# Output and down projections with the activations stationary and 512 weight columns moving, in a two-layer hybrid decoder trunk

## The chip, the cores and the metric

The kernel runs on one core of one Trainium2 chip. The metric is the device time of one execution in microseconds (us); the time before is the median of three runs. A difference of less than about 0.3% (7.8 us here) is about what such a measurement cannot tell from no change.

## What is computed

Two layers over 256 tokens of 2048 channels. Each layer mixes tokens (three groups of heads behind one input projection and one output projection), then channels (a gated MLP with a short causal convolution). The two projections of this case are the ones that bring a sub-layer's result back to 2048 channels, each followed by an RMSNorm over the channels, a gate and the residual sum:

```python
mix = jnp.concatenate([o_a, o_b, o_c], axis=-1) @ w_out[l]          # (256, 2048) @ (2048, 2048)
x = x + gate1 * rmsnorm(mix, mix_post_norm[l])
h = rmsnorm(x, ffn_pre_norm[l]) * (1.0 + scale2) + shift2
u = causal_dwconv(h @ ffn_w_up[l], ffn_conv[l]) + ffn_conv_b[l]
gate_br, up = u[..., :D_FF], u[..., D_FF:]
y = (jax.nn.gelu(gate_br, approximate=True) * up) @ ffn_w_down[l]   # (256, 5632) @ (5632, 2048)
x = x + gate2 * rmsnorm(y, ffn_post_norm[l])
```

## The kernel before

**Layout and products.** Activations lie with channels on the 128 partitions and the 256 tokens along the free dimension; `x` is 16 such tiles (k = 0 to 15) in the buffers S1 and S3. Every large product is float32 made of three products of rounded halves (float32r): a weight `w` is split into `wh` and `wl`, an activation into `hh` (or `mh`) and `hl` (or `ml`), and `mm3` (L262 to L266) adds `wh·hh` (L264), `wh·hl` (L265) and `wl·hh` (L266) in PSUM. The weights are the stationary operand (128x128 blocks) and the 256 tokens move (258 where two columns for the shift ride along). So each weight block costs three loads of the stationary operand and three products of 256 columns.

**The stream of weights.** All weights come as one stream of chunks of 512 KB (128 partitions x 1024 floats), issued from the SP queue (L179) into 6 raw buffers, in the order in which `build_stream` lists them. Between them stand the chunks of the modulation's weights (`ada`, L181), which VectorE multiplies and sums (L208). A weight chunk is split by ScalarE (L202, the rounded half) and VectorE (L203, the rest) into one of 4 `hl` buffers, two chunks ahead of its use (`piece`, L544, with LOOK = 2). Epilogues are generators that advance one step per chunk (`tick`).

**The two projections.** The output projection (in `mix_layer`) runs in two halves of the sum: first the channels 8 to 15 (attention), then 0 to 7 (the delta rule), 16 chunks each; a chunk is one column of blocks (`ct`), eight blocks deep. The down projection (in `ffn_layer`) comes in three groups of 16, 16 and 12 channel tiles of the MLP, each after the up-projections that feed it; a group has 16 columns of blocks with two chunks each (8 and 8, or 8 and 4 blocks), in the order of `down_order`, which puts the first chunks of four columns ahead. `m_gen` (L761) moves each finished column from PSUM: ScalarE copies it (L766) or VectorE adds it to what is there (L768). In the last group it also squares it for the norm (ScalarE L452, the sum of squares on GpSimd L453; the last two columns apart, L777 and L780).

**The joint.** After a projection, `post` (L485) sums the squares over channels with products by a column of ones (L460), forms mean and epsilon (VectorE L468), takes the power -1/2 on GpSimd (L260), and spreads it over the partitions with a product (L308). Then `step(i)` makes, for each of the 16 tiles, `m *= rs` (VectorE L518), `x += gate * m` (VectorE L521), the next `hh` (ScalarE L525) and `hl` (VectorE L528). `h_first` (L543) calls the steps while it multiplies the first four tiles of the next projection, 48 products per four k. There are three such joints, and a tail after the last projection, where L510 and L511 do the two sums over up to four tiles at once and SP stores them (L512).

What stands in which order on an engine is decided when the program is built: the code gives the order of emission, and a scheduler moves instructions of one engine past each other within the limits of their dependences.

## Time and profile before

| | |
|---|---|
| three runs | 2584.64, 2586.0 (the median) and 2592.09 us |
| profiled execution | span 2591.2 us from the first to the last instruction; its own time is not listed beside the runs', and its span lies 5.2 us above their median and within their range |
| TensorE matmul busy, weight load busy | 2494.2 and 2416.5 us (96% and 93%) |
| VectorE, ScalarE, GpSimd busy | 2051.5, 1385.0, 176.4 us (79%, 53%, 7%) |
| mean granted TensorE clock | 0.989 |
| moved by DMA | 630.48 MB, mean 243 GB/s |

Busy time of matmuls overlaps from one to the next, and their ends are modelled; the distance from one start to the next is what a product costs in a row of them. In a timeline row the first number is the start, the second the time, in us; "x2" counts equal instructions that follow each other, and a bracket at the end gives the idle time before and what ended it. In a table of stretches a row has the stretch, its length, and then for PE, PEld, DVE, ACT and POOL the busy time in us with the count of instructions; the last three numbers are the granted share of the TensorE clock, the busy share of the DMA engines and the GB/s they moved. PE is TensorE, PEld its weight load, DVE VectorE, ACT ScalarE, POOL GpSimd, SP the queue that issues the transfers.

### The profile page before, as it was taken

The numbers are of one execution on the slowest core, as the hardware profiler recorded it, in microseconds if no ns is written. First come the engines' busy times: TensorE is split into PE (matmuls) and PEld (weight loads), VectorE is DVE, ScalarE is ACT, GpSimd is POOL, SyncE is SP. The second block draws the span as 40 slices with busy tenths as digits, with TensorE's granted clock in tenths as the row PEclk, the third lists the DMA queues.
The fourth block names the chain that finished last, engine by engine and source line by source line (L and its number), as shares of the span: only waits on it lengthen the run. The fifth ranks groups of instructions, "written<-read, shape, count | busy, mean of one in ns | idle before, by whom it ended". The sixth has DMA issues, their size and how long they took to land.

```text
span 2591.2 us, 51150 instructions
## 1 busy us (share of the span) xinstructions
PE 2494.2 (96%) x20144; PEld 2416.5 (93%) x20144; DVE 2051.5 (79%) x3828; ACT 1385.0 (53%) x2357; POOL 176.4 (7%) x208
## 2 busy tenths in 40 slices
PE   3999999989999999999989999999999999999997
PEld 2999978989999999999989998898899999999997
DVE  7888988899876888688869887678977467766764
ACT  2465356456553555345547556664656455644654
POOL 0001100230000000000121110002100000000001
PEclk9999999999999999999999999999999999999998
DMA  9997878958888888888747765587566666666653
GB/s 366 342 336 223 294 262 268 338 196 284 266 270 282 262 264 265 282 272 268 259 158 264 242 208 183 170 278 276 187 212 206 210 208 208 210 208 208 211 165 122
DMA packets 175268, 630.48 MB, mean 243 GB/s; under 512 B 19905, under 2 KB 20305, under 8 KB 174769
## 3 DMA queue, kind: packets, MB, share of 16 engines
q1 hardware_dynamic: 170784, 612.44, 71.8%
q0 software_dynamic: 4096, 14.62, 1.7%
q8 instruction: 158, 2.59, 0.4%
q14 instruction: 84, 0.69, 0.1%
q10 hardware_dynamic: 146, 0.14, 0.0%
HBM read 618.73 MB, written 8.39 MB: 242 GB/s over the span
## 4 chain that ended last, share of the span: by engine, by line
PE 61%; DMA 16%; DVE 14%; issue 7%; ACT 2%; POOL 0%; DVEq 0%; POOLq 0%; ACTq 0%
PE mm L264 17%; PE mm L266 17%; PE mm L265 17%; DMA raw<-ada 15%; DVE hl L203 5%; DVE raw L208 3%; PE mm L578 2%; DVE ys L655 1%; ACT hl L202 1%; DVE hl L528 1%; PE sd L1279 1%; DVE S L521 1%; PE sd L303 1%; ACT ys L652 1%; PE mm L1177 0%
## 5 line engine op out<-in xcount | busy, mean ns | idle before, releaser
L264 PE MATMUL mm<-hh,hl 128*128 128x258 f32 (+1 forms) x4056 | 1154.0, 286 | 33.4 <-ACT hh L433 25.2
L266 PE MATMUL mm<-hh,hl 128*128 128x258 f32 (+1 forms) x4056 | 1149.8, 284 | 11.8 <-DVE hl L203 10.8
L265 PE MATMUL mm<-hl 128*128 128x256 f32 x4056 | 1147.5, 283 | 10.3 <-DVE hl L528 7.8
L203 DVE TENSOR_TENSOR hl<-raw,hl 128x1024 fp32r<-128x1024 f32 (+1 forms) x774 | 929.7, 1205 | 231.3 <-ACT hl L202 230.1
L202 ACT CAST hl<-raw 128x1024 fp32r<-128x1024 f32 (+1 forms) x774 | 794.2, 1028 | 586.2 <-PE mm L266 469.2
L264 PEld LDWEIGHTS mm<-hh,hl 128*128 128x128 f32 x4056 | 763.8, 189 | 40.2 <-ACT hh L433 25.5
L266 PEld LDWEIGHTS mm<-hh,hl 128*128 128x128 f32 x4056 | 773.2, 191 | 21.4 <-DVE hl L203 18.2
L265 PEld LDWEIGHTS mm<-hl 128*128 128x128 f32 x4056 | 774.5, 191 | 18.8 <-DVE hl L528 13.9
L208 DVE SCALAR_TENSOR_TENSOR raw<-raw,c_bc 128x1024 f32<-128x1024 f32 x384 | 475.5, 1242 | 176.0 <-DMA raw<-ada 162.5
L266 PE MATMUL mm<-mh,hl 128*128 128x256 f32 x1920 | 544.9, 284 | 5.4 <-DVE hl L203 5.3
L265 PE MATMUL mm<-ml,hl 128*128 128x256 f32 x1928 | 546.4, 283 | 0.1
L264 PE MATMUL mm<-mh,hl 128*128 128x256 f32 x1920 | 545.6, 284 | 0.1
L266 PEld LDWEIGHTS mm<-mh,hl 128*128 128x128 f32 x1920 | 368.9, 192 | 7.2 <-DVE hl L203 7.2
L265 PEld LDWEIGHTS mm<-ml,hl 128*128 128x128 f32 x1928 | 370.6, 192 | 0.6 <-issue 0.3
L264 PEld LDWEIGHTS mm<-mh,hl 128*128 128x128 f32 x1920 | 368.9, 192 | 1.8 <-issue 1.4
L655 DVE SCALAR_TENSOR_TENSOR ys<-us,fvec,ys 128x255 f32<-128x255 f32 x352 | 168.6, 481 | 9.2
L651 ACT ACTIVATE us<-us,c 128x256 f32<-128x256 f32 x176 | 89.1, 507 | 130.9 <-DVE c L634 129.6
L453 POOL TENSOR_TENSOR t<-t 128x256 f32<-128x256 f32 x97 | 90.9, 937 | 929.8 <-ACT t L452 929.0
L652 ACT ACTIVATE ys<-us,fvec 128x256 f32<-128x256 f32 x176 | 105.6, 601 | 5.3
L633 DVE TENSOR_TENSOR us<-mm,rs 128x256 f32<-128x256 f32 x174 | 73.0, 420 | 19.7 <-PE mm L266 19.6
L316 ACT CAST mh<-ys 128x256 fp32r<-128x256 f32 x88 | 35.4, 404 | 76.2 <-DVE ys L1366 76.2
L452 ACT ACTIVATE t<-S 128x256 f32<-128x256 f32 x97 | 39.5, 410 | 50.1 <-DVE S L768 49.0
(339 smaller groups left out, 1798.5 us busy)
## 6 DMA issues: line engine op xcount, KB each, us to landing
raw<-ada SPq DMA_DIRECT2D x384, 512.0 KB, 4.7
raw<-up SPq DMA_DIRECT2D x352, 512.0 KB, 4.5
raw<-w_in SPq DMA_DIRECT2D x176, 512.0 KB, 4.8
raw<-down SPq DMA_DIRECT2D x160, 512.0 KB, 4.5
raw<-w_out SPq DMA_DIRECT2D x64, 512.0 KB, 5.3
raw<-down SPq DMA_DIRECT2D x32, 256.0 KB, 3.4
raw<-uq SPq DMA_DIRECT2D x6, 512.0 KB, 5.8
S<-xt SPq DMA_DIRECT2D x4, 512.0 KB, 10.0
```

The costliest lines, as they stand in the source:

```text
L202: nc.scalar.copy(out=hi[:, :n], in_=raw[:, :n])
L203: nc.vector.tensor_tensor(out=lo[:, :n], in0=raw[:, :n], in1=hi.bitcast(F32)[:, :n], op=ALU.subtract)
L208: self.ada_ins = nc.vector.scalar_tensor_tensor(out=raw, in0=raw, scalar=1.0, in1=self.c_bc[:, hf * 1024:(hf + 1) * 1024], op0=ALU.mult, o ...
L264: mm(ps, wh, hh, start=start, stop=False)
L265: mm(ps[:, :256], wh, hl, start=False, stop=False)
L266: mm(ps, wl, hh, start=False, stop=stop)
L453: nc.gpsimd.tensor_tensor(out=self.sqacc, in0=self.sqacc, in1=t, op=ALU.add)
L578: self.nc.tensor.matmul(ps, lhsT=cv[0][0][:, k, :], rhs=self.x[kk // 8][:, kk % 8, :], start=i == 0 and k == 0, stop=kk == 15)
L633: nc.vector.tensor_tensor(out=out[r], in0=ps[r, :256], in1=self.rs[r], op=ALU.mult)
L651: nc.scalar.activation(out=u, in_=u, func=AF.Identity, bias=b)
L652: nc.scalar.activation(out=y, in_=u, func=AF.Identity, scale=taps[:, n - 1:n], bias=bias)
L655: nc.vector.scalar_tensor_tensor(out=y[:, s:], in0=u[:, :S - s], scalar=taps[:, n - 1 - s:n - s], in1=y[:, s:], op0=ALU.mult, op1=ALU.add)
```

## The change

The weights become the moving operand and the activations the stationary one. `mm3t` multiplies, for each half T of the tokens, a 128x128 block of activations (`hi`, `lo`) by 512 columns of one row of weight blocks: three products of 512 columns per T in place of six of 256 (two column blocks, three each, per 256 columns of weights; over the same chunk 12 products in place of 24, with the same number of columns). The result is by tokens: `m[:, T, :]` has tokens on the partitions and 2048 channels along the free dimension.

- A chunk is now two blocks deep and 512 columns wide (`w_out` and `down` are laid out anew on the host, still 4 KB per partition), and the last group of the down projection has 24 full chunks in place of 16 full and 16 half ones.
- `m_gen` moves 128x512 at once; in the last group ScalarE squares each and sums it in the same instruction (`accum_out`), so that the sums of squares need neither GpSimd nor the products by ones.
- In `post` VectorE reduces the eight sums, GpSimd takes the power as before, and VectorE makes two diagonal matrices of the result (`dg`).
- `turn(k)` multiplies a 128x128 block of `m` by the diagonal in plain float32: this brings channels back to the partitions and applies the norm at once, into PSUM, two k to a buffer. `add(k)` does `x += gate * turned`; the separate `m *= rs` is gone, and in the tail each k is added alone.

```diff
+    def mm3t(self, pss, wh, wl, hi, lo, start, stop):
+
+        mm = self.nc.tensor.matmul
+        for T, ps in enumerate(pss):
+            sl = slice(T * 128, T * 128 + 128)
+            mm(ps, hi[:, sl], wh, start=start, stop=False)
+            mm(ps, hi[:, sl], wl, start=False, stop=False)
+            mm(ps, lo[:, sl], wh, start=False, stop=stop)
...
-        c = self.rs_cols([(sq, slice(0, 128)) for sq in [self.sqacc, *self.last_sqs.values()]], D)
+        c = self.col()
+        nc.vector.tensor_reduce(out=c, in_=self.msq.rearrange("p (t j) -> p t j", t=2), op=ALU.add, axis=mybir.AxisListType.X)
+        self.rs_ins = nc.vector.tensor_scalar(out=c, in0=c, scalar1=1.0 / D, scalar2=EPS, op0=ALU.mult, op1=ALU.add)
+        r = self.col()
+        self.rpow(r, c, 0)
+        dg = self.tmp()
+        for T in range(2):
+            nc.vector.tensor_scalar(out=dg[:, T * 128:T * 128 + 128], in0=self.cs("ident"), scalar1=r[:, T:T + 1], scalar2=None, op0=ALU.mult)
...
-        ps = self.sd(256)
-        self.bcast_cols(ps, c)
+        def turn(k):
+
+            if k % 2 == 0:
+                pss[k // 2] = self.sd()
+            for T in range(2):
+                o = k % 2 * 256 + T * 128
+                nc.tensor.matmul(pss[k // 2][:, o:o + 128], lhsT=m[:, T, k * 128:k * 128 + 128], rhs=dg[:, T * 128:T * 128 + 128],
+                                 start=True, stop=True)
+
+        def add(k):
+            xk = x[k // 8][:, k % 8, :]
+            return nc.vector.scalar_tensor_tensor(out=xk, in0=pss[k // 2][:, k % 2 * 256:k % 2 * 256 + 256], scalar=g[:, k:k + 1],
+                                                  in1=xk, op0=ALU.mult, op1=ALU.add)
...
         def step(i):
             if i < KT:
-                nc.vector.tensor_tensor(out=m[:, i, :], in0=m[:, i, :], in1=ps, op=ALU.mult)
+                turn(i)
             k = i - 1
             if 0 <= k < KT:
-                ins = nc.vector.scalar_tensor_tensor(out=x[k // 8][:, k % 8, :], in0=m[:, k, :], scalar=g[:, k:k + 1],
-                                                     in1=x[k // 8][:, k % 8, :], op0=ALU.mult, op1=ALU.add)
+                ins = add(k)
...
+    def by_tokens(self, ids, act, m, prev, last):
+
+        n = len(act)
+        for j in range(4):
+            pss = [self.mm(512) for _ in range(2)]
+            for i, c in enumerate(ids[j]):
                 def fn(cv):
                     wh, wl = cv[0]
+                    for k in range(2):
+                        kk = 2 * i + k
+                        self.mm3t(pss, wh[:, k, :], wl[:, k, :], *act[kk], kk == 0, kk == n - 1)
+                self.piece([c], fn)
+                if i == len(ids[j]) - 1:
+                    for T in range(2):
+                        self.spawn(self.m_gen(m, j, T, pss[T], prev, last))
                 self.tick()
...
+            self.sq_ins = nc.scalar.activation(out=ps, in_=m[:, T, sl], func=AF.Square, accum_out=self.msq[:, T * 4 + j:T * 4 + j + 1])
...
-                d = {}
-                for ct, i in down_order():
-                    k = f0 + 8 * i
-                    d[ct, i] = add(io["down"][l, ct, :, k:min(k + 8, f1), :])
-                downs.append(d)
+                downs.append([[add(io["down"][l, j, :, k:k + 2, :]) for k in range(f0, f1, 2)] for j in range(4)])
```

**The order on the engines.** On TensorE, at the end of the last down projection, before (a name is the tile written, then what it is made of: `mm` a PSUM buffer, `mh`/`ml` the halves of an activation tile, `hl` a weight buffer):

```order
L264 MATMUL mm_30209<-mh10_29425,hl_30190 128x256
L265 MATMUL mm_30209<-ml10_29426,hl_30190 128x256
L266 MATMUL mm_30209<-mh10_29425,hl_30190 128x256
L264 MATMUL mm_30209<-mh11_29440,hl_30190 128x256
L265 MATMUL mm_30209<-ml11_29441,hl_30190 128x256
L266 MATMUL mm_30209<-mh11_29440,hl_30190 128x256
L460 MATMUL sd_30254<-cst_87,t_29617 128x1
```

and with the change:

```order
L265 MATMUL mm_26928<-hl_26979,mh11_26604 128x512
L266 MATMUL mm_26928<-hl_26979,mh11_26604 128x512
L267 MATMUL mm_26928<-hl_26979,ml11_26605 128x512
L265 MATMUL mm_26929<-hl_26979,mh11_26604 128x512
L266 MATMUL mm_26929<-hl_26979,mh11_26604 128x512
L267 MATMUL mm_26929<-hl_26979,ml11_26605 128x512
```

Two blocks of one chunk took six products of 256 columns; now one row of blocks takes six of 512, three into each of two PSUM buffers (one per half of the tokens), and nothing by ones follows.

On VectorE, at the first joint (after the first output projection), before, from the last two columns' sum to the first steps:

```order
L768 TENSOR_TENSOR S_5382<-part,mm 128x256 x2
L780 TENSOR_TENSOR t<-S_5382 128x256
L397 TENSOR_TENSOR hh<-mod,hh 128x16
L203 TENSOR_TENSOR hl<-raw,hl 128x1024
L468 TENSOR_SCALAR c<-sd 128x1 x2
L203 TENSOR_TENSOR hl<-raw,hl 128x1024
L518 TENSOR_TENSOR S_5382<-S_5382,sd 128x256 x2
L521 SCALAR_TENSOR_TENSOR S_5383<-S_5382,gcol,S_5383 128x256
L518 TENSOR_TENSOR S_5382<-S_5382,sd 128x256
L521 SCALAR_TENSOR_TENSOR S_5383<-S_5382,gcol,S_5383 128x256
L528 SCALAR_TENSOR_TENSOR hl<-S_5383,acol,hh 128x256
```

and with the change (L196 is the former L203, L523 `add`, L548 the former L528):

```order
L797 TENSOR_TENSOR S_5174<-part,mm 128x512 x2
L498 TENSOR_REDUCE c<-c 128x2
L398 TENSOR_TENSOR hh<-mod,hh 128x16
L499 TENSOR_SCALAR c<-c 128x2
L196 TENSOR_TENSOR hl<-raw,hl 128x1024
L504 TENSOR_SCALAR t<-cst,c 128x128 x2
L196 TENSOR_TENSOR hl<-raw,hl 128x1024 x2
L523 SCALAR_TENSOR_TENSOR S_5175<-sd,gcol,S_5175 128x256 x2
L196 TENSOR_TENSOR hl<-raw,hl 128x1024
L548 SCALAR_TENSOR_TENSOR hl<-S_5175,acol,hh 128x256
L523 SCALAR_TENSOR_TENSOR S_5175<-sd,gcol,S_5175 128x256
```

The sums by `rs` (L518) are gone; two splits of weights now stand between the diagonal (L504) and the first `add`, and a third right behind it. At the second and third joints it is one split ahead of the first `add`, and one behind.

## Rows read from the trace of the kernel before

**Rows 1.** The page's busy times and its chain of waits by engine.

```profile
PE 2494.2 (96%) x20144; PEld 2416.5 (93%) x20144; DVE 2051.5 (79%) x3828; ACT 1385.0 (53%) x2357; POOL 176.4 (7%) x208
...
PE 61%; DMA 16%; DVE 14%; issue 7%; ACT 2%; POOL 0%; DVEq 0%; POOLq 0%; ACTq 0%
```

**Rows 2.** Table of stretches: four of the six down projections.

```profile
735.00:827.60 92.60, 92.31 (x770) 92.10 (x769) 62.13 (x81) 41.22 (x55) 0.00 (x0) 1.00 0.84 279
...
1253.00:1327.30 74.30, 70.74 (x578) 70.53 (x577) 47.90 (x76) 36.26 (x56) 12.98 (x16) 0.98 0.71 233
...
2275.60:2367.70 92.10, 92.10 (x770) 92.10 (x769) 52.92 (x63) 34.94 (x35) 0.00 (x0) 1.00 0.68 209
...
2504.80:2573.80 69.00, 69.00 (x578) 69.00 (x577) 33.35 (x50) 38.13 (x62) 9.63 (x13) 1.00 0.46 138
```

**Rows 3.** Timeline of TensorE in a down projection, ten products that follow each other.

```profile
2299.74 0.28 PE L264 MATMUL mm<-mh,hl 128*128 128x256 f32 x1
...
2300.82 0.28 PE L264 MATMUL mm<-mh,hl 128*128 128x256 f32 x1
```

**Rows 4.** Timeline of TensorE in the latent keys' and values' projection, first layer.

```profile
350.96 0.39 PE L1217 MATMUL sd<-hl,ml 128*128 128x512 f32 x1
...
352.12 0.40 PE L1219 MATMUL sd<-hl,ml 128*128 128x512 f32 x1
```

**Rows 5.** The same in the second layer.

```profile
1627.78 0.28 PE L265 MATMUL mm<-ml,hl 128*128 128x256 f32 x1
...
1628.38 0.40 PE L1217 MATMUL sd<-hl,ml 128*128 128x512 f32 x1
...
1629.31 0.28 PE L264 MATMUL mm<-ml,hl 128*128 128x256 f32 x1
```

**Rows 6.** Timeline of TensorE, plain float32 products.

```profile
190.09 0.59 PE L835 MATMUL sd<-w,cst 128*128 128x256 f32 x2
190.52 0.38 PE L836 MATMUL sd<-w,cst 128*128 128x128 f32 x2
190.74 0.39 PE L837 MATMUL sd<-w,cst 128*128 128x128 f32 x2
```

**Rows 7.** Table of stretches: the second halves of the two output projections.

```profile
488.00:531.90 43.90, 43.46 (x362) 43.25 (x362) 41.34 (x58) 22.55 (x31) 15.57 (x13) 1.00 0.93 333
...
1750.00:1800.30 50.30, 49.31 (x404) 48.49 (x403) 43.46 (x60) 22.50 (x32) 13.65 (x13) 1.00 0.92 327
```

**Rows 8.** Waits in the first layer's last down projection: total, times, longest.

```profile
PE mm L266 <- DVE hl L203: 3.6, 1, 3.6
```

**Rows 9.** Table of stretches: the first joint up to its first product, and a part behind it.

```profile
531.90:539.30 7.40, 2.94 (x19) 2.47 (x17) 5.06 (x12) 2.00 (x5) 1.61 (x1) 0.71 0.53 169
...
552.00:573.00 21.00, 17.85 (x130) 15.98 (x130) 21.00 (x31) 11.44 (x22) 7.69 (x9) 1.00 0.44 130
```

**Rows 10.** Timeline of the first joint.

```profile
534.66 1.61 POOL L260 TENSOR_TENSOR c<-c,pw 128x2 f32<-128x2 f32 x1 [3.97 <-DVE c L468]
536.32 1.22 PE L308 MATMUL sd<-cst,c 128*128 128x128 f32 x4 [2.00 <-POOL c L260]
537.58 0.75 DVE L518 TENSOR_TENSOR S<-S,sd 128x256 f32<-128x256 f32 x2 [1.87 <-PE sd L308]
```

**Rows 11.** Groups by line and shape: xcount | busy us, mean ns.

```profile
L203 DVE TENSOR_TENSOR hl<-raw,hl 128x1024 fp32r<-128x1024 f32 x742 | 907.7, 1227 | 225.1 <-ACT hl L202 223.9
...
L203 DVE TENSOR_TENSOR hl<-raw,hl 128x512 fp32r<-128x512 f32 x32 | 22.1, 692 | 6.2 <-ACT hl L202 6.2
...
L202 ACT CAST hl<-raw 128x512 fp32r<-128x512 f32 x32 | 19.7, 619 | 16.0 <-PE mm L266 15.2 <-ACT hl L202 0.5 <-ACT t L452 0.3
...
L443 DVE TENSOR_SCALAR t<-t,c 128x128 f32<-128x128 f32 x16 | 3.9, 284 | 4.0 <-POOL c L260 4.0
```

**Rows 12.** Timeline of VectorE in the tail.

```profile
2578.42 2.35 DVE L510 TENSOR_TENSOR S<-S,sd 128x1024 f32<-128x1024 f32 x2 [2.10 <-PE sd L308]
...
2587.09 0.75 DVE L511 TENSOR_TENSOR S<-S,S 128x256 f32<-128x256 f32 x2
```

93 lines of the change are left out of this document (30 added, 63 removed).

## The prediction, made before the changed kernel was run

> **What bounds the kernel now.** I read the page first, then the table of stretches, then the timelines inside a stretch. The page says that TensorE is busy for 96% of the span and holds 61% of the chain that ended last [rows 1]; since matmul busy time overlaps itself, this alone does not show a bound. The table does. In the down projections, three per layer, TensorE's busy time fills the stretch, while VectorE and ScalarE have a third or more to spare and the transfers run below 280 GB/s [rows 2]. There are 768 products in a full group and 576 in the last one, so a full group of the second layer takes 92.1 / 768 = 0.120 us per product. The timeline shows that pace as a steady beat: nine steps from 2299.74 to 2300.82 are 0.120 each [rows 3]. Nothing is waited for there. What changes the step changes the time.
>
> The joints are bounded otherwise. Some 7.4 us pass between a projection's last product and the next projection's first, in which TensorE does 2.9 us of work, at a granted clock of 0.71 [rows 9], so more than half of that stretch at the lower of its two levels, 1.2 GHz. Later, while the next operand is made tile by tile, VectorE is busy for 21.0 of 21.0 us and TensorE for 17.85 [rows 9]. So in that part VectorE is the bound.
>
> **The products.** The change takes 24 products of 256 columns from each chunk and puts 12 of 512 in their place; a pair of the old ones costs 2 x 0.1198 = 0.2396 us. The price of a new one stands in this trace, since the values of the latent attention are already made in just this way: halves of an activation stationary, 512 converted weight columns moving. Five steps from 350.96 to 352.12 make 0.232 us each [rows 4]; in the second layer four steps from 1628.38 to 1629.31 make 0.2325, and the five 256-column products right ahead of them, from 1627.78 to 1628.38, 0.120 each [rows 5]. I take 0.232, a saving of 0.0076 us per pair. As to the bounds: the single steps that I add up lie between 0.22 and 0.24; at 0.24 nothing is saved, and 0.22 would save 0.02. Plain float32 products tell the same small story from another side: one with 256 columns takes (190.52 - 190.09) / 2 = 0.215 us, two of 128 take 0.22 [rows 6].
>
> The down projections have 4224 such products, 2112 pairs: 2112 x 0.0076 = **-16 us** (0 at 0.24, -41 at 0.22). The output projections have 1536, 768 pairs: -6 if TensorE alone set their pace. But in their second halves VectorE is busy for 41.3 of 43.9 us in the first layer and 43.5 of 50.3 in the second, and the DMA engines for 0.92 to 0.93 of the time [rows 7]. I give them half: **-3 us** (0 to -6).
>
> The Trainium skill ("TensorE: Matmul & The Clock Gate", Back-to-back issue gap) gives the gap of a product at full clock as its columns over 2.4 GHz plus 2.5 ns, so that joining two saves only the 2.5 ns. The rows differ from it: both lengths run slower than it says, 256 columns by some 10 ns. By the rule's difference alone the down projections would save 5 us in place of 16.
>
> **Moving the results out** gets cheaper and stays off the path: eight moves of 128x512 per group, at about 0.69 us by a VectorE instruction of that shape [rows 11], in place of sixteen of 128x256. They are covered by VectorE's free third [rows 2]; without that cover eight of them would cost 5.5 us per group. Of the 13 GpSimd additions per last group none is left. The SP queue keeps its transfers and bytes, except that 16 pairs of a full and a half chunk become 24 full ones. In the first layer's last group the half chunks are consumed faster than they arrive with the modulation's chunks between them: one wait of 3.6 us on a split that stood behind it on VectorE [rows 8]. Equal chunks should spare part of it: **-2 us** (0 to -3.6).
>
> **The joints**, three of them. What goes: on VectorE 16 sums by `rs` per joint, two of which take 0.75 us [rows 10], so 6 us in the stretch where VectorE is the bound; on TensorE the two spreading products with their loads, 1.22 us [rows 10]. What comes: first, a longer start. The last sum is 128x512, 0.69 in place of about 0.4 us; the square stands on ScalarE, 0.62 us for that width [rows 11]; the diagonal takes two VectorE instructions of 0.28 [rows 11]; GpSimd's 1.61 us [rows 10] stays. The tiny products by ones go, which pays for most of that. Then the splits ahead of the first `add`, 1.23 us each [rows 11]: two at the first joint, one at the others, of which the turning products hide about 0.7. I put the first product with the new operand 1.7 us later at the first joint and 0.5 later at the others. These splits are moved, not added: what is done early need not be done in the full stretch. Second, 32 plain products of 128 columns on TensorE at 0.11 us each [rows 6], 3.5 us at the upper clock and twice that at the lower. Twelve stand ahead of the first product, beside the splits; the other twenty, 2.2 us, fall into the stretch where TensorE is idle for 3.1 us [rows 9], which hides them as long as VectorE is late there. With VectorE 6 us shorter TensorE comes within 1 or 2 us of being the bound itself, so most of the 6 us is not to be had. I put each joint at -1 us (-4 to +4): **-3 us**.
>
> **The tail.** VectorE's two sums ran from 2578.42 to 2587.84, 9.4 us [rows 12]. Sixteen single `add` take some 0.4 each, 6 us; TensorE, back at the lower clock, needs 2 x 0.22 per tile, 7 us in all, and becomes the slower one. That is 2.4 less, and the start is 0.3 later: **-2 us** (-3 to +1).
>
> **Sum:** -16 - 3 - 2 - 3 - 2 = -26. The profiled span of 2591.2 would become 2565; that execution lies 5.2 us over the median of the runs, 2586.0, and I hold the difference against the median: **2560 us**.
>
> **The rivals.** (A) *The columns set the pace, not the products.* 512 columns then cost what two times 256 cost, 0.24, and only stall, joints and tail are left, -7: 2579. For it: the two prices differ by only 3%, and one step in rows 4 and 5 is as long as 0.24. Against it: the mean of nine steps. The Trainium skill's rule for the gap (the page and section above) is a case of this kind: by its 2.5 ns per pair the estimate would be 2574. (B) *A fixed cost per product was hidden in the steady beat*, and 512 columns run at the shortest step seen, 0.22: -41 - 7 for the down projections, stall, joints and tail, and another -8 in the output projections, half of their 768 x 0.02: 2530. For it: a steady beat without a free step; against it the same mean. (C) *The joints take it back.* If the turning products run at the lower clock, where the granted 0.71 puts the joint [rows 9], 32 of them cost 7 us, and the twenty late ones 4.4 where 3.1 were idle; with the later start and twelve early ones uncovered this makes +5 per joint in place of -1: 2578. Against it: the clock is back at 1.00 in the stretch where most of them fall. (D) *Slower: the moving weights collide with their own making.* The 512 moving columns are read from buffers beside which ScalarE and VectorE write the next chunk, and the nine measured steps come from two single chunks, not from a full stream. At 0.25 the 2880 products cost 0.0104 x 2880 = +30 us, less 7: 2609. It decides from about 0.245, where (0.245 - 0.2396) x 2880 = 15.6 us outweigh the 7 and the 0.3% bound. Against it: the same chunks are read as stationary blocks now, beside the same writes, without a wait.
>
> **How the numbers follow.** About 0.3%, 7.8 us, is what a measurement of this kernel can tell from no change. My forecast (a step of 0.226 to 0.237, joints about even) has 0.62, with a range of its own of 2548 to 2572. A has 0.16, half of it beyond the bound; B 0.10, C 0.08, half beyond the bound, D 0.04. Faster: 0.62 + 0.08 + 0.10 + 0.04 = 0.84; within 0.3%: 0.12; slower: 0.04. The range leaves out the outer part of B, part of C and all of D: 2540 to 2579.
>
> **What the profile will show.** A down projection's full group of the second layer should take 384 x 0.232 = 89 us in place of 92.1, with steps of 0.23; if it takes 92, A holds, if 84.5, B. The span from a projection's last product to the next one's first should be near 9 us at the first joint and 8 at the others; VectorE's full stretch behind it should be shorter or TensorE full in it. The plain products of the joint should stand 0.11 us apart, or 0.22 where the clock is low. The wait of 3.6 us should be shorter, and VectorE's last sums in the tail should take 7 us in place of 9.4. I am wrong if the step of the new products is not what rows 4 and 5 show, or if a joint's first tiles take over 4 us longer than now.

## The result, and the profile after

The changed kernel takes 2549.2 us in the median of four runs (2547.18 to 2564.59); the kernel before, run beside it, takes 2586.2. The ratio is 0.986 with a 95% interval of 0.9831 to 0.9889: faster by 37 us, 11 more than forecast, inside the range of 2540 to 2579. On another chip the same kernel came to 2553.6 us and 0.9886 (0.9868 to 0.9905).

The page: TensorE's weight loads fall by 141 us of busy time, while its products are still busy for 97% of the span; GpSimd falls from 176 to 123 us, and TensorE holds 64% of the chain that ended last instead of 61% [rows 1].

```profile
PE 2464.5 (97%) x17456; PEld 2275.2 (89%) x17456; DVE 2014.4 (79%) x3724; ACT 1374.0 (54%) x2299; POOL 122.8 (5%) x156
...
PE 64%; DMA 16%; DVE 11%; issue 6%; ACT 2%; POOL 0%; DVEq 0%; POOLq 0%; ACTq 0%
```

The table of stretches, with the columns of [rows 2]: two down groups of the first layer (the first and the last), the same of the second layer, the second halves of the output projections (they answer to [rows 7]), the first joint and the stretch behind it (they answer to [rows 9]), and the tail.

```profile
729.50:819.40 89.90, 88.69 (x385) 71.30 (x384) 61.10 (x81) 40.81 (x47) 0.00 (x0) 1.00 0.85 284
1242.30:1308.90 66.60, 65.64 (x290) 53.56 (x288) 44.02 (x60) 31.22 (x44) 1.69 (x3) 1.00 0.78 258
2240.40:2327.20 86.80, 86.80 (x385) 71.92 (x384) 50.25 (x55) 35.17 (x35) 0.00 (x0) 1.00 0.72 217
2464.40:2529.50 65.10, 65.10 (x290) 53.88 (x288) 31.72 (x34) 27.19 (x36) 0.00 (x0) 1.00 0.45 130
487.00:528.00 41.00, 39.65 (x173) 31.94 (x172) 35.28 (x50) 18.43 (x26) 0.00 (x0) 1.00 0.95 342
1729.00:1771.70 42.70, 42.70 (x191) 35.34 (x189) 34.58 (x48) 19.59 (x28) 0.00 (x0) 1.00 0.96 360
528.00:538.60 10.60, 5.52 (x26) 5.12 (x25) 8.18 (x16) 5.79 (x12) 2.21 (x2) 0.72 0.56 200
551.00:573.00 22.00, 20.90 (x178) 20.70 (x177) 19.74 (x28) 11.78 (x20) 9.46 (x9) 1.00 0.60 193
2529.50:2546.70 17.20, 9.64 (x66) 8.90 (x64) 8.90 (x22) 1.40 (x4) 0.69 (x1) 0.90 0.31 122
```

The second layer's groups still have TensorE full from end to end; they are simply shorter: 86.8 us for 384 products, 65.1 for 288. The first layer's have small holes now (88.69 of 89.90 busy), which before were nearly absent (92.31 of 92.60 [rows 2]).

Where the profiled spans' 44.5 us (2591.2 to 2546.7) went, stage by stage, in both traces. A group or an output projection is taken from its first product to the start of its last; a joint with its stage runs from there to the end of the up-projections or input projection behind it:

| stage | before | after | difference |
|---|---|---|---|
| six down groups | 512.8 | 485.3 | -27.5 |
| two output projections | 199.6 | 188.5 | -11.1 |
| three joints, each with the stage behind it | 688.4 | 686.5 | -1.9 |
| tail | 17.4 | 17.2 | -0.2 |
| the rest, which the change does not touch | | | -3.8 |

The rest is mostly one stretch of the second layer's attention (74.6 to 70.4 us), which comes to anything from 70.4 to 74.6 in the runs of this study. The two profiled executions lie on opposite sides of their medians, so 44.5 between them is 37 between the medians. The rows of joints and tail are one execution each, too: in another execution of the same changed kernel (the run `again` of experiment 7) the joints with their stages come to 689.9 us and the tail to 18.6, so that for these two rows the traces show no change either way.

**The step.** Timeline of TensorE in a steady stretch of a down projection, seven products in a row:

```profile
2299.80 0.39 PE L266 MATMUL mm<-hl,mh 128*128 128x512 f32 x1
...
2301.16 0.39 PE L266 MATMUL mm<-hl,mh 128*128 128x512 f32 x1
```

Six steps in 1.36 us: 0.2267 each, not 0.232. The same timeline in the first layer, from a wait for a split on:

```profile
738.72 0.50 PE L266 MATMUL mm<-hl,mh 128*128 128x512 f32 x1 [0.47 <-DVE hl L196]
739.06 0.39 PE L267 MATMUL mm<-hl,ml 128*128 128x512 f32 x1
739.29 0.39 PE L265 MATMUL mm<-hl,mh 128*128 128x512 f32 x1
...
740.45 0.39 PE L267 MATMUL mm<-hl,ml 128*128 128x512 f32 x1
```

Here the six steps from 739.06 to 740.45 make 0.232, the price that [rows 4, 5] had shown. Those rows were the first products behind another kind of product, as these are the first behind a wait; later the steps settle at 0.2267 (from 740.67 on in this stretch).

**The first joint.** TensorE and VectorE, from the last product of the output projection to the first of the up projection:

```profile
528.01 0.39 PE L267 MATMUL mm<-hl,ml 128*128 128x512 f32 x1
533.48 5.49 PE L518 MATMUL sd<-t,S 128*128 128x128 f32 x24 [5.08 <-DVE t L504]
538.62 0.99 PE L256 MATMUL mm<-hh,hl 128*128 128x258 f32 x3
```

```profile
533.53 2.35 DVE L196 TENSOR_TENSOR hl<-raw,hl 128x1024 fp32r<-128x1024 f32 x2
535.80 0.87 DVE L523 SCALAR_TENSOR_TENSOR S<-sd,gcol,S 128x256 f32<-128x256 f32 x2
536.59 1.22 DVE L196 TENSOR_TENSOR hl<-raw,hl 128x1024 fp32r<-128x1024 f32 x1
537.72 0.48 DVE L548 SCALAR_TENSOR_TENSOR hl<-S,acol,hh 128x256 fp32r<-128x256 f32 x1
```

The twelve turning products (two records each) take 5.1 us, 0.43 each; the granted clock is 0.72 over the joint and 0.50 over the turns themselves (533.5 to 538.6). VectorE does two splits ahead of its first sum and a third ahead of its first difference. From last to first product it is 10.6 us here, 9.5 and 10.3 at the other joints; before it was 7.3 to 7.4. The stages behind give it back, 4.7, 1.1 and 4.4 us shorter. Two things differ there. From 551 us on TensorE is busy for 20.9 of 22.0 us, where it was busy for 17.85 of 21.0 [rows 9]. And in the 12 us right behind the joint the clock is higher; before and after:

```profile
539.30:552.00 12.70, 12.24 (x72) 11.44 (x72) 11.63 (x24) 7.66 (x18) 5.67 (x7) 0.76 0.13 45
```

```profile
538.60:551.00 12.40, 12.40 (x103) 12.40 (x103) 10.64 (x20) 8.18 (x18) 6.59 (x8) 0.96 0.45 151
```

Before, the clock stood at 0.50 for the first 6 us of that stretch, with TensorE and VectorE both busy throughout; now the low time falls on the turns ahead of it. What each of the two is worth was not separated.

**VectorE beside no GpSimd.** Groups of VectorE by line in the second layer's output projection, second half: the splits and the modulation products took 1.28 and 1.46 us in the kernel before and take 1.22 now. Before:

```profile
L203 DVE TENSOR_TENSOR hl<-raw,hl 128x1024 fp32r<-128x1024 f32 x16 | 20.5, 1282 | 0.0
L208 DVE SCALAR_TENSOR_TENSOR raw<-raw,c_bc 128x1024 f32<-128x1024 f32 x13 | 19.0, 1464 | 3.8 <-DMA raw<-ada 3.8
```

and after:

```profile
L196 DVE TENSOR_TENSOR hl<-raw,hl 128x1024 fp32r<-128x1024 f32 x14 | 17.1, 1223 | 0.4 <-ACT hl L195 0.4
...
L200 DVE SCALAR_TENSOR_TENSOR raw<-raw,c_bc 128x1024 f32<-128x1024 f32 x12 | 14.7, 1223 | 2.1 <-DMA raw<-ada 2.1
```

### The profile page after: what moved, and what is told of

Its sections match the earlier page's. It is cut to its first block, busy times and chain, and to the rows that moved or that the text cites. A ratio compares the mean times of both kernels' runs of the same rounds, so it can differ in the third digit from the quotient of the medians.

```text
span 2546.7 us, 45378 instructions
## 1 busy us (share of the span) xinstructions
PE 2464.5 (97%) x17456; PEld 2275.2 (89%) x17456; DVE 2014.4 (79%) x3724; ACT 1374.0 (54%) x2299; POOL 122.8 (5%) x156
## 4 chain that ended last, share of the span: by engine, by line
PE 64%; DMA 16%; DVE 11%; issue 6%; ACT 2%; POOL 0%; DVEq 0%; POOLq 0%; ACTq 0%
DMA raw<-ada 15%; PE mm L256 12%; PE mm L258 12%; PE mm L257 12%; PE mm L265 6%; PE mm L266 6%; PE mm L267 6%; DVE hl L196 4%; DVE raw L200 3%; PE mm L598 2%; DVE ys L675 1%; PE sd L518 1%; ACT hl L195 1%; PE sd L304 1%; PE sd L1299 1%
## 5 line engine op out<-in xcount | busy, mean ns | idle before, releaser
L195 ACT CAST hl<-raw 128x1024 fp32r<-128x1024 f32 x758 | 791.3, 1048 | 668.8 <-PE mm L258 276.5
L196 DVE TENSOR_TENSOR hl<-raw,hl 128x1024 fp32r<-128x1024 f32 x758 | 925.7, 1226 | 227.5 <-ACT hl L195 226.1
L200 DVE SCALAR_TENSOR_TENSOR raw<-raw,c_bc 128x1024 f32<-128x1024 f32 x384 | 469.3, 1225 | 167.5 <-DMA raw<-ada 155.3
L266 PE MATMUL mm<-hl,mh 128*128 128x512 f32 x960 | 376.0, 392 | 4.8 <-DVE hl L196 4.6
L265 PE MATMUL mm<-hl,mh 128*128 128x512 f32 x960 | 374.6, 391 | 0.0
L267 PE MATMUL mm<-hl,ml 128*128 128x512 f32 x960 | 373.9, 389 | 0.0
L266 PEld LDWEIGHTS mm<-hl,mh 128*128 128x128 f32 x960 | 180.2, 188 | 48.6 <-DVE hl L196 12.3
L265 PEld LDWEIGHTS mm<-hl,mh 128*128 128x128 f32 x960 | 180.2, 188 | 38.5 <-issue 1.4
L267 PEld LDWEIGHTS mm<-hl,ml 128*128 128x128 f32 x960 | 180.3, 188 | 36.9
L252 POOL TENSOR_TENSOR c<-c,pw 128x2 f32<-128x2 f32 x26 | 26.9, 1040 | 1180.2 <-DVE c L499 919.3
L1383 ACT ACTIVATE ys<-ys 128x256 f32<-128x256 f32 x88 | 36.6, 416 | 44.9 <-DVE ys L675 44.2
```

What stands on the lines that cost most here:

```text
L195: nc.scalar.copy(out=hi[:, :n], in_=raw[:, :n])
L196: nc.vector.tensor_tensor(out=lo[:, :n], in0=raw[:, :n], in1=hi.bitcast(F32)[:, :n], op=ALU.subtract)
L200: self.ada_ins = nc.vector.scalar_tensor_tensor(out=raw, in0=raw, scalar=1.0, in1=self.c_bc[:, hf * 1024:(hf + 1) * 1024], op0=ALU.mult, o ...
L265: mm(ps, hi[:, sl], wh, start=start, stop=False)
L266: mm(ps, hi[:, sl], wl, start=False, stop=False)
L267: mm(ps, lo[:, sl], wh, start=False, stop=stop)
```

## Experiments

My theory after the result, worked out from the two steps (0.2267 us for 512 columns and 0.120 for 256, so 0.107 for 256 columns more): every float32r product costs about 13 ns besides its columns, so that 512 columns in place of two times 256 save 13 ns per pair and nothing else in the change matters much. A line through two points always fits; experiment 2 adds a third. The rival: the exchange of the roles (fewer moves out, no GpSimd sums) is what gained. Then: why do the joints and the tail give nothing, and why did the first layer's groups gain less than the second's?

**1. Half the width (w256).**

```diff
-        for j in range(4):
-            pss = [self.mm(512) for _ in range(2)]
+        for j in range(NJ):          # NJ = D // W, W = 256
+            pss = [self.mm(W) for _ in range(2)]
```

> Roles as in the changed kernel (activation stationary, weight columns moving, norm by tokens, turned back by the diagonal), but 256 weight columns per product instead of 512: twice as many products, eight blocks of columns instead of four. Theory (a product has a fixed cost of about 13 ns beside its columns, 119.8 = 256 x 0.4167 + 13.1 and 226.7 = 512 x 0.4167 + 13.3, and the width is the whole gain): steps of 0.120 us, the second layer's full down group back at 92 us (86.8 in the changed kernel), its last one at 69, the whole 2880 x 0.0129 = 37 us over the changed kernel, less some 6 us where the first layer's waits hide it: 2579 to 2587. Rival (it is the exchange of the roles that gains: fewer moves out, a freer VectorE and GpSimd): steps of 0.113, groups stay at 87, time 2549 to 2555.

Measured: 2580.0 us, ratio to before 0.997 (0.9957 to 0.9984). Table of stretches, a full down group and the last one of the second layer:

```profile
2263.40:2355.40 92.00, 92.00 (x770) 92.00 (x769) 52.02 (x63) 34.93 (x35) 0.00 (x0) 1.00 0.67 207
...
2492.50:2561.50 69.00, 69.00 (x578) 69.00 (x576) 33.39 (x42) 29.08 (x52) 0.00 (x0) 1.00 0.41 123
```

Both groups are back to what [rows 2] had. All down and output stages together take 712.5 us, against 712.4 before and 673.8 in the changed kernel. The width is the gain there. The exchange of roles alone moves nothing in the sum of these stages: the two output projections get shorter (103.7 and 93.6 us for 105.1 and 94.5), the first layer's down groups longer by about as much. The 8 us that remain against the kernel before (2588.0 in that session) lie elsewhere, a part of them at the first joint and its stage (198.7 us for 202.9).

**2. A quarter of the width (w128)**, the same edit with W = 128.

> The same with 128 weight columns per product, four times as many products. Theory of the fixed cost: a step of 128 x 0.4167 + 13.2 = 66.5 ns, the second layer's full down group 1536 x 0.0665 = 102 us, the whole 2880 x (4 x 0.0665 - 0.2267) = 113 us over the changed kernel, about 2660. Rival (the step has a floor, because a block of 128 columns has to be loaded as stationary for each product and that takes as long as 256 columns move): 0.12 per product, a full group near 184 us, the whole some 730 us longer, near 3280.

Measured: 3874.7 us, ratio 1.4963 (1.49 to 1.5026). A stretch of the first layer's second down group and one of the second layer's first, then the product with which TensorE goes on in the former after a wait, and two products from the latter:

```profile
1473.60:1784.10 310.50, 308.36 (x1446) 308.21 (x1446) 69.80 (x104) 32.84 (x33) 0.00 (x0) 0.50 0.27 85
3088.00:3249.40 161.40, 161.40 (x1448) 161.40 (x1447) 41.35 (x38) 37.96 (x61) 0.00 (x0) 1.00 0.37 113
```

```profile
1475.72 0.33 PE L268 MATMUL mm<-hl,mh 128*128 128x128 f32 x1 [2.42 <-ACT mh L320]
...
3149.89 0.28 PE L270 MATMUL mm<-hl,ml 128*128 128x128 f32 x1
...
3150.78 0.28 PE L269 MATMUL mm<-hl,mh 128*128 128x128 f32 x1
```

Eight steps in 0.89 us are 0.111 each at the upper clock. "Columns and 13 ns" fails below 256 columns: 128 cost nearly as much as 256 (0.120), so there is a floor near 0.11, as the rival said (whether it is the load of the stationary block or the rate of narrow products, these rows do not tell). Between 256 and 512 the theory agrees with the steps from which it was worked out and with experiment 1; for other widths it is not shown. Both forecasts of the total were far too short, as neither had the clock: in five of the eight down and output stages it is granted at 0.50 for all or most of the time, and such a full group takes 320 us in place of 171. In each of the five TensorE first waited for an operand, 1.6 to 2.4 us in four (the line at 1475.72 is one), 7.0 in the output projection of the first layer (which had a low stretch before that, too, behind three waits of 0.8 to 0.9 us); the clock fell then, and came back only when the stage's products had ended, though TensorE was busy. The three stages without such a wait stayed at 1.00.

**3. Keep TensorE at work through the joints (warm).** Unread products stand behind the last one:

```diff
+                    if last and j == 3 and i == len(ids[j]) - 1:
+                        spare = self.sd()
+                        with self.tc.issue_after(self.pe_ins.ins):
+                            for _ in range(22 if self.w_last + 1 < len(self.widx) else 14):
+                                self.nc.tensor.matmul(spare, act[0][0][:, :128], wh[:, 1, :], start=True, stop=True)
```

> The changed kernel with products that nobody reads between a projection's last product and the first turning product: 22 of 512 columns at each of the three joints, 14 at the tail (their sums go to a spare PSUM buffer). They keep TensorE at work until the diagonal is ready. Theory (the turns are slow because TensorE stood still and runs at the lower clock): the granted clock of the joints rises from 0.72 to 0.9 or more, a turning product takes 0.11 to 0.22 us instead of 0.43, twelve of them end 2.5 us earlier; first products 1 to 1.8 us earlier at the first joint and 0.5 to 1 at the others, the tail's first sums 1.4 us earlier: 4 to 6 us faster than the changed kernel, 2543 to 2546. Rival (VectorE, with the splits ahead of its first sums, sets the start, and the slow turns only fill its time): the turns get faster and the first products come at the same time, gain at most 2 us, all of it in the tail: 2547 to 2549. Second rival (the turns are slow for another reason, their loads or plain float32): clock up, turns still 0.4 apart.

Measured: 2553.9 us, ratio 0.9857 (0.9838 to 0.9876), beside 0.986 and 0.9886 of the changed kernel. Stretches of the first and third joint, and TensorE's timeline in the third (L787 are the unread products):

```profile
532.90:541.10 8.20, 8.10 (x49) 6.86 (x47) 5.76 (x13) 5.39 (x11) 1.53 (x1) 1.00 0.51 185
...
1780.00:1787.80 7.80, 7.80 (x49) 6.90 (x47) 5.71 (x13) 4.49 (x10) 1.59 (x1) 1.00 0.33 101
```

```profile
1780.21 5.15 PE L787 MATMUL sd<-hl,mh 128*128 128x512 f32 x22
1785.20 2.84 PE L518 MATMUL sd<-t,S 128*128 128x128 f32 x24
1787.79 0.48 PE L256 MATMUL mm<-hh,hl 128*128 128x258 f32 x2
```

The clock stays at 1.00, the twelve turns take 2.6 us (0.22 each) in place of 5.1, and the joints 8.2, 7.8 and 7.8 us in place of 10.6, 9.5 and 10.3. So the turns were slow because of the clock, and they did stand on the path. But only the third joint clearly keeps its gain (joint and stage together 196.6 in place of 198.9). The first gives it back behind (200.9 for 201.4). For the second it cannot be told: 286.4 for 286.2, but 290.3 in the other execution of the changed kernel. The tail takes 15.6 us in place of 17.2 (18.6 in the other execution). That is some 4 us of stages, too little for the total to tell; the total lies above both expected ranges, in a session in which the kernel before took 2588.0. The second rival (slow for another reason than the clock) is out: with the clock up the turns halve.

**4. Fewer turns ahead of the first product (few).**

```diff
-            while n < 4 * kg + 6:
+            while n < (4 * kg + 6 if kg else 4):
                 step(n)
...
                 for k in range(4):
                     kk = 4 * kg + k
+                    while n < kk + 4:
+                        step(n)
+                        n += 1
```

> The changed kernel with four tiles turned ahead of the first product of the next projection instead of six (the other turns stand between the products of the first four k), and with the split of the third chunk behind VectorE's second difference instead of its second sum. Theory (four of the twelve turns, at 0.36 to 0.43 us each, and one split of 1.22 us stand on the path to the first products): first product 1.4 to 1.7 us earlier at each of the three joints, TensorE full behind it as now, 3 to 5 us in all: 2544 to 2546. Rival (VectorE's work up to the last of the 16 tiles sets the stretch; TensorE only waits later): the wait of 1.38 us on a difference near the end of the stretch grows by what the first product gains, and the time stays at 2548 to 2550.

Measured: 2552.9 us, ratio 0.9862 (0.9847 to 0.9877), outside both ranges, but not to be told from the changed kernel's 0.986. The joints shrink to 8.9, 8.6 and 8.6 us, as expected, and the stages behind grow: 204.0, 285.6 and 199.6 for joint and stage in place of 201.4, 286.2 and 198.9. The end of the first of these stages shows a new wait: with another order of emission the product that sums the squares stands ahead of others, and TensorE waits for GpSimd's last sum.

```profile
563.31 0.28 PE L257 MATMUL mm<-hl 128*128 128x256 f32 x1
565.03 0.61 PE L461 MATMUL sd<-cst,t 128*128 128x1 f32 x4 [1.44 <-POOL t L454]
```

This does not tell how much of an earlier start VectorE alone would allow; experiment 6 does.

**5. GpSimd's sums put back (gps).**

```diff
+            for _ in range(2 if j < 3 else 1):
+                nc.gpsimd.tensor_tensor(out=self.tmp(), in0=m[:, T, j * 512:j * 512 + 256], in1=m[:, T, j * 512 + 256:j * 512 + 512], op=ALU.add)
```

> The changed kernel with GpSimd sums as the kernel before had them, in the last group of each projection: 14 additions of 128x256 on tiles of the result, which nobody reads. Theory (GpSimd's sums made VectorE's work longer in the kernel before, 1.28 us per split and 1.46 per modulation product in the second halves of the output projections, where the changed kernel shows 1.22 and 1.22; TensorE sets the pace there all the same): the modulation products beside the sums take 1.4 us or more again, the splits 1.27 or more, the output projections' second halves stay within 1 us, the whole at 2547 to 2552. Rival (VectorE set the pace in those halves, and its relief is what gave them their full gain): the second layer's half grows by 3 us or more, the whole by 5 to 10: 2554 to 2560.

Measured: 2554.1 us, ratio 0.9883 (0.986 to 0.9906), beside 2553.6 us of the changed kernel in the same session (experiment 7), so that the total decides nothing; the stages do. VectorE's groups in the second layer's output projection, second half:

```profile
L196 DVE TENSOR_TENSOR hl<-raw,hl 128x1024 fp32r<-128x1024 f32 x12 | 16.1, 1339 | 0.0
L200 DVE SCALAR_TENSOR_TENSOR raw<-raw,c_bc 128x1024 f32<-128x1024 f32 x11 | 15.0, 1367 | 2.3 <-DMA raw<-ada 2.3
```

Beside the sums the same instructions take 1.34 and 1.37 us instead of 1.22. The output projections take 104.0 and 88.3 us in place of 101.2 and 87.3: 3.8 us in all, so that their relief was worth something, mostly in the first layer. In the second it is 1 us, against the 3 or more that the rival wanted: TensorE sets the pace there.

**6. The same sums taken from the joints (warm_nosum)**, on top of the kernel of experiment 3.

```diff
-            t = self.tmp()
-            nc.scalar.activation(out=t, in_=src, func=AF.Square)
-            nc.gpsimd.tensor_tensor(out=self.sqacc, in0=self.sqacc, in1=t, op=ALU.add)
+            self.sqacc = self.tmp()
+            nc.scalar.activation(out=self.sqacc, in_=src, func=AF.Square)
```

> The kernel with the unread products at joints and tail, and without GpSimd's sums of squares in the stages that follow the joints: the sum of squares of the new residual is left out (its last tile's squares alone stand for it, so the scale of the norm is another); ScalarE's squares and all else stay. Theory (beside GpSimd's sums VectorE's 128x1024 work takes 1.75 us instead of 1.22, which makes VectorE late there, and so the first layer's joints gave back what the earlier first product had gained): VectorE's splits all near 1.22, the waits of 1.1 and 1.5 us at the end of the stretch gone, the stage after the first joint at 189 to 190.5 us instead of 192.7, the one after the second 276 or less instead of 278.6: 3 to 6 us faster than with the sums, 2546 to 2551. Rival (the number of VectorE's instructions sets that stretch): stages within 1 us of 192.7 and 278.6.

Measured: 2540.4 us, ratio 0.9842 (0.9828 to 0.9857), below the expected range. VectorE's groups behind the first joint, with the sums and without:

```profile
L196 DVE TENSOR_TENSOR hl<-raw,hl 128x1024 fp32r<-128x1024 f32 x10 | 14.2, 1431 | 0.0
L548 DVE SCALAR_TENSOR_TENSOR hl<-S,acol,hh 128x256 fp32r<-128x256 f32 x16 | 9.9, 643 | 0.0
...
L523 DVE SCALAR_TENSOR_TENSOR S<-sd,gcol,S 128x256 f32<-128x256 f32 x13 | 5.8, 473 | 0.0
```

```profile
L196 DVE TENSOR_TENSOR hl<-raw,hl 128x1024 fp32r<-128x1024 f32 x11 | 13.4, 1222 | 2.3 <-ACT hl L195 2.3
L547 DVE SCALAR_TENSOR_TENSOR hl<-S,acol,hh 128x256 fp32r<-128x256 f32 x12 | 5.5, 477 | 0.1
...
L522 DVE SCALAR_TENSOR_TENSOR S<-sd,gcol,S 128x256 f32<-128x256 f32 x10 | 4.3, 476 | 0.0
```

Beside GpSimd a split takes 1.43 us in the mean and a difference 0.64; without, 1.22 and 0.48. The sum that reads PSUM takes 0.47 either way. The first joint and its stage come to 196.6 us in place of 200.9, the second to 283.8 in place of 286.4. With the sums TensorE waits for 2.8 us behind the first joint, for halves of the next operand from VectorE and ScalarE and for splits; without them it does not wait. So behind the first joint it is VectorE, slowed by GpSimd's sums, that takes back an earlier first product. Behind the second the same is likely but not shown, since 2.6 us lie within what two executions of one kernel differ by there.

**7. Why the first layer's groups are longer: look further ahead (look3), one landing buffer more (raw7).**

```diff
-                self.piece([c], fn)
+                self.piece([c], fn, look=3 if n > 8 else LOOK)
```

> The changed kernel with the chunks of the down projections split three chunks ahead of their products instead of two. In the first layer the three groups take 3.1, 3.2 and 1.5 us longer than the same groups of the second layer, 7.8 in all, in waits of 0.45 to 1.35 us on a split by VectorE. Theory (a split comes late now and then, and one more chunk of about 2.7 us ahead takes that up): the groups come down to 87, 87 and 65.5, 4 to 8 us faster than the changed kernel, 2541 to 2545. Rival (the splits stand behind modulation products on VectorE whose transfers are late, as its 28.6 us of waiting for them in the first group say, and looking further ahead in the same ring of six chunks brings no transfer sooner): groups within 1 us of now, 2547 to 2551.

```diff
-RAW = 6
-TMP = 8
+RAW = 7
+TMP = 6
```

> The changed kernel with seven landing buffers for weight chunks instead of six (and, to make room, six in place of eight small work tiles and two in place of three of 384 columns). Theory (in the first layer the modulation's chunks are late because a transfer starts only when a buffer comes free, so VectorE waits for them and the splits behind it come late): one more transfer under way, waits of the first layer's down and up stages shrink, 5 to 15 us faster than the changed kernel, 2534 to 2544. Rival (the transfers run at the pace of the queue, or the smaller pools of work tiles cost as much): 2546 to 2555.

Measured: 2553.6 and 2557.6 us, ratios 0.9885 (0.9867 to 0.9902) and 0.9896 (0.9875 to 0.9918), beside 0.9886 of the changed kernel in the same session. The first layer's groups took 90.7, 90.6 and 67.2 us with the longer look, 90.1, 90.4 and 67.7 with seven buffers. Neither helps; the total of raw7 lies above both of its ranges, and its smaller pools of work tiles, which made room for the buffer, may have cost what it gave.

> The changed kernel once more, on the same chip as the three others, so that differences of a few microseconds can be told: 2547 to 2553 if the chip is like the one before.

Measured: 2553.6 us (2547.23 to 2560.28), ratio 0.9886 (0.9868 to 0.9905); groups of 88.4, 90.1 and 66.7.

**8. No modulation chunks among the down projections' (nomod).**

```diff
-                downs.append([[add(io["down"][l, j, :, k:k + 2, :]) for k in range(f0, f1, 2)] for j in range(4)])
+                downs.append([[(add if l else self.add_w)(io["down"][l, j, :, k:k + 2, :]) for k in range(f0, f1, 2)] for j in range(4)])
```

> The changed kernel with no modulation chunks among the chunks of the first layer's down projections; all 128 of that sub-layer stand among its 168 chunks of the up projection instead of 250 of both. Theory (the first layer's down groups take 234 ns per product instead of 226 because splits on VectorE stand behind modulation products whose transfers are late): groups of 86.8, 86.8 and 65.1 us instead of 89.9, 90.0 and 66.6, with 227 ns from the first products on; the up stages, where VectorE has less to spare, grow by as much or more: 2545 to 2565. Rival (the weight transfers themselves are late in the first layer): groups stay within 1 us of 90, 90 and 66.6.

Measured: 2568.9 us, ratio 0.9946 (0.9927 to 0.9965), 4 us above the expected range. Two of the first layer's groups:

```profile
727.30:814.10 86.80, 86.80 (x385) 71.90 (x385) 44.69 (x45) 38.59 (x42) 0.00 (x0) 1.00 0.65 208
...
1254.10:1319.20 65.10, 65.10 (x290) 53.90 (x288) 33.47 (x38) 30.32 (x41) 1.68 (x3) 1.00 0.59 194
```

They are now those of the second layer to a tenth. The modulation's chunks make the difference, and they cost more elsewhere: the second and third up stage (the up-projections ahead of the second and third group) take 203.8 and 148.7 us in place of 190.7 and 141.6. How they do it stands in the changed kernel's own trace, VectorE in the first layer's first group (729.5 to 819.4): it waits 28.6 us for modulation transfers, and the splits that stand behind these products are what TensorE waits for.

```profile
L200 DVE SCALAR_TENSOR_TENSOR raw<-raw,c_bc 128x1024 f32<-128x1024 f32 x17 | 20.8, 1225 | 28.7 <-DMA raw<-ada 28.6
```

**9. A version made of these (warm_again, shift).** The kernel of experiment 3 once more; and with the modulation's chunks moved the other way, from the up stages to the down groups:

> The kernel with the unread products at joints and tail once more, timed on the same chip as the two others: if the second layer's third joint (2.3 us) and the tail (1.6 us or more) are gains that stay, 2545 to 2552, 3 to 5 us below the changed kernel; the first two joints give nothing, since VectorE is late there.

```diff
-            spread((FFN_N[l > 0], min(192 * (l + 1) + ADA_FFN, len(ada)) - pos[0]))
+            n = min(192 * (l + 1) + ADA_FFN, len(ada)) - pos[0]
+            spread(*(((FFN_N[1], n),) if l else ((56, 17), (32, 26), (64, 23), (32, 26), (48, 17), (24, 19))))
```

> The kernel with the unread products at joints and tail, and the first layer's 128 modulation chunks of the feed-forward part moved the other way: 57 among the up projection's 168 chunks and 71 among the down projections' 88, where an even spread puts about 84 and 44. From the run without modulation chunks in the down projections: about 44 chunks fewer gained 3.1 + 3.2 + 1.5 us there (0.18 each), and as many more in the up stages cost 0.9 + 13.1 + 7.1 us (0.48 each). Theory (in the up stages VectorE is the bound, in the down projections it is idle for a third and only transfers have to fit, at 58 chunks per 87 us as many as the second layer's output projection takes without a wait): up stages 1 to 3, 4 to 6 and 2 to 4 us shorter (189 to 191, 184 to 186, 138 to 140), down groups 1 to 3 us longer each, 4 to 9 us faster than with the even spread, 2542 to 2547. Rival (the transfers do not fit: the down groups grow by 0.3 us or more per chunk moved there, 27 chunks, 8 us): as long as with the even spread or longer, 2549 to 2556.

Measured: 2550.7 us, 0.9877 (0.9861 to 0.9892), for the first, again not to be told from the changed kernel by its total, with the same 8.2, 7.8, 7.8 and 15.6 us at joints and tail. For the second 2566.9 us, 0.9934 (0.9918 to 0.995). The first layer's second up stage and the down group ahead of it:

```profile
726.50:820.00 93.50, 88.59 (x385) 71.47 (x384) 72.57 (x99) 40.85 (x47) 0.00 (x0) 1.00 0.90 320
820.30:1018.10 197.80, 186.87 (x1536) 183.70 (x1535) 152.22 (x262) 105.44 (x154) 0.00 (x0) 1.00 0.70 233
```

The group grows by 3.6 us, a little more than the theory allowed, but the up stage, with fewer chunks than before, grows too, by 7. My straight line of 0.18 and 0.48 us per chunk was wrong: both directions from the even spread are worse. In that up stage VectorE waits 40.8 us for modulation transfers where it waited 22.4 in the changed kernel, and TensorE 10.9 us for splits in place of 2.0; why fewer transfers come later stays open.

No version here beats the changed kernel by a margin that its total shows. The one without sums lies 9 to 13 us below it but leaves out work; what it would cost to do that sum elsewhere was not tried.

## Why the prediction was right, and where its sizes were off

The direction, the bound and the mechanism held: the second layer's down projections were bound by TensorE's step alone, the first layer's nearly so, and longer products took less time for the same columns. By its own sign of being wrong (a step that is not the one of [rows 4, 5]) the prediction missed in the size of that step. By its own steps:

- **Products, -16.** The mis-sized term. I took 0.232 from the first steps of a burst [rows 4, 5]; a long stream settles at 0.2267. Per pair that is 0.2396 - 0.2267 = 0.013 us in place of 0.0076; the second layer's 1056 pairs gained 14.4 us, 0.0136 each. Rival B (0.22) had seen a fixed cost per product, and put it too high; A (0.24, only the columns count) is ruled out by the steps and by w256, where the same columns in twice as many products cost 39 us in these stages, and D (0.25) by the steps.
- **The rule of the Trainium skill** ("TensorE: Matmul & The Clock Gate", Back-to-back issue gap), 2.5 ns saved per pair, disagrees with the trace: 13 ns. That section of the Trainium skill gives the rule for a product by itself and a lower figure, 131 ns, for 512 columns in a stream; the stream here shows 226.7.
- **Output projections, half of the saving.** They gained 11.1 us; 2880 pairs at 0.013 make 37 for all, of which these have 10. Halving was near for the first layer and wrong for the second: 384 pairs per layer are worth 5 us, and from w256 to the changed kernel, which differ in the width, the first layer's projection goes from 103.7 to 101.2 us, the second's from 93.6 to 87.3. VectorE's 43 us of 50 [rows 7] did not set the pace in the second. The other 2.3 us come with the roles (w256 beside the kernel before); experiment 5 puts GpSimd's relief, which I had not priced, at 3.8.
- **The stall in the last group, -2.** It gained 3.8: that group's excess over the second layer's was 5.3 us and is 1.5. I had priced the wait of 3.6 us alone; the granted clock of that group, 0.98 over 74.3 us [rows 2], makes another 1.5, by my estimate (0.02 x 74.3), and it is 1.00 now.
- **Missing: what is late next.** The first layer's two full groups now take 3.0 and 3.2 us longer than the second layer's, where it was 0.5 and 0.6. With chunks used up faster, splits stand behind modulation products whose transfers are late (experiment 8): +5 that no step of mine had.
- **Joints, -3.** They gave -1.9 in the profiled executions, near the forecast by luck, since the sizes were others. The price of a turn was half of what it is: I read the records of [rows 6] as products, but each product stands in two records there (the kernel issues one product from each of the three lines), so that one of 128 columns takes 0.22 us at the upper clock, not 0.11. The changed kernel shows 0.43 at the lower clock and 0.22 at the upper (experiment 3), and 32 turns are 7 us at the upper clock, not 3.5. The start is longer by 3.2, 2.2 and 2.9 us, where I put 1.7 and 0.5: twelve turns at 0.43 us stood on the path, which I had said would run beside the splits, and a third split stands ahead of the first difference. Rival C had the lower clock right and the same halved price (0.22 there), and the consequence wrong: the stages behind are shorter by 4.7, 1.1 and 4.4, as TensorE stands idle less in them and the clock is back earlier.
- **Tail, -2.** It gave -0.2. VectorE's sums take 8.6 us, not 7 (2535.06 to 2543.66), and wait 1.97 us for the first turns, again at the lower clock; the turns had the same halved price. With the clock kept up (experiment 3) the tail gains 1.6.

```profile
2535.06 0.88 DVE L523 SCALAR_TENSOR_TENSOR S<-sd,gcol,S 128x256 f32<-128x256 f32 x2 [1.97 <-PE sd L518]
...
2543.18 0.48 DVE L523 SCALAR_TENSOR_TENSOR S<-sd,gcol,S 128x256 f32<-128x256 f32 x1 [0.81 <-PE sd L518]
```

## What to carry to other kernels

Where TensorE's steady step is the bound, take the price of a step from a long run of equal products, not from the first few of a burst; here the difference was two fifths of the gain per pair (0.0053 of 0.0129 us). Before a row becomes a price, count how many records the profile has for one product; here that halved the price of the turns. After shortening the bound, ask at each place which stream is consumed faster now: its transfers and the instructions queued behind them are the next wait. And an engine that seems idle and harmless beside the bound, as GpSimd with its sums, can lengthen the work of its neighbour: compare the mean time of one instruction between stretches with and without it.

## What I had not expected of the hardware

- **A step is not linear in the columns.** At the upper clock 0.111 us for 128 columns, 0.120 for 256, 0.2267 for 512, all float32r with a new stationary block each time.
- **The first products of a burst are slower**, 0.232 against 0.2267, for some six products behind a wait or a change of kind.
- **The lower clock with a full engine.** In the run with 128 columns the granted clock stood at 0.50 for the rest of a group, 310 us, with TensorE busy for 308 of them. Ahead of it came a group's up projection and 10 us of the narrow products, at 1.00, and then a wait of 2.4 us for an operand, behind which the clock fell; it came back within 10 us of the next 258-column products. All five stages in which TensorE waited so (1.6 to 7.0 us, experiment 2) went this way, and the second layer's down groups of the same products, which had none, ran at 1.00 throughout. With products of 256 columns a wait of 3.6 us [rows 8] brought the clock down as well, but not for the rest of its group (0.98 over the whole). Why it does not come back among the narrow ones stays open.
- **GpSimd beside VectorE.** A 128x1024 split takes 1.22 us alone, up to 1.76 beside a GpSimd sum (run warm, behind the first joint); instructions with one operand in PSUM (0.47 us) are not touched. The Trainium skill ("SBUF — State Buffer", Who interferes with whom) says that a VectorE instruction with two SBUF inputs contends with a GpSimd instruction that reads SBUF, and one with at most one, outside its 2-port modes, does not; the rows agree.
